# Two-layer decoder trunk: places of 96 and 64 slots in turn, and a branch for each overfull expert

## Chip, cores and metric

The kernel runs on one core of a Trainium2 chip. The metric is the device time of one execution in microseconds (us), the median of several runs. TensorE (PE) multiplies matrices, VectorE (DVE), ScalarE (ACT) and GpSimd (POOL) do the element-wise work, SyncE (SP) issues nearly all loads, and sixteen DMA engines move the data.

## What is computed

Two pre-norm residual layers over 256 tokens of width 1024, in float32. Layer 0 has two kinds of attention and a dense SwiGLU; layer 1 has sliding-window attention beside a short convolution, and then eight experts, of which each token takes two. The change touches only these experts:

```python
def moe_swiglu(x, w_router, w_gate, w_up, w_down):
    xt = x.reshape(B * S, D)
    logits = (xt @ w_router).astype(jnp.float32)
    top_vals, top_idx = lax.top_k(logits, TOP_K)
    top_w = jax.nn.softmax(top_vals, axis=-1)
    ...
    for e in range(N_EXPERTS):
        y = y + gates[:, e:e + 1] * swiglu(xt, w_gate[e], w_up[e], w_down[e])
```

Each expert has three matrices of 1024 x 3584 in float32. 256 tokens with two experts each make 512 pairs, 64 per expert on the mean.

## The kernel before

The first part (layer 0 and the attention of layer 1) is not touched. The last part, the expert stage, starts near 495 us and ends the program.

**Places.** The stage works through eight places, 0 to 7. A place has a fixed number of slots, `CAPS`: 96, 64, 96, 96, 64, 96, 96, 64. A slot is a column of a matrix into which a token is gathered. Expert 0 always has place 0; the other seven are ranked by their token counts on the chip (`arrange`), and `RANKS` tells which rank goes to places 1 to 7, so that the places of 64 get the smaller experts. `read_counts` loads into registers which expert stands in each place (on SyncE, for the addresses of the weights) and, on each engine, `t.over`, the largest number of tokens beyond a place's slots.

**Work of a place.** The place's tokens are gathered by a matmul with a one-hot matrix (L1090, tile tt). The hidden width of 3584 is done in two halves, r = 0 and 1. Each half takes two loads of the gate matrix, two of the up matrix (L1138, tile mm) and two of the down matrix (L1181 and L1185, tiles y and yo): twelve loads of 3584 KB per place. TensorE works on blocks of 32 slots, of which four matmuls stand side by side in its columns. A place of 96 has three blocks, a place of 64 two. In the down part the first two blocks go into y with 512 columns a matmul; the third goes into yo with 256, and a place of 64 has no yo. L1165 transposes the hidden values (once per half for the first two blocks, once more for the third), L1213 and L1214 scatter the result back to the tokens.

**Order.** `experts` writes a plan: gate of one half, then the down part of the half before, then up, with the small steps (gather of the next group, transposes, scatter) as fillers between. TensorE runs in just this order; the other engines' order is the scheduler's.

**Buffers.** All weights go through four raw buffers of 28 KB per partition, in turn. When TensorE has finished a load, the next is issued on SyncE's queue into the freed buffer, so at most four loads are under way or waiting to be used. The first four are issued before the stage starts.

**End.** After the last place come the final norm and two output transfers (L1285). Then stand two bodies behind branches (L1292): if `t.over` is above 0, all eight places are run again with 96 slots each for the tokens left over, and if it is above 96 once more.

Of the kernel before, what the change touches and what calls it, by code (L numbers as in the profile page):

```python
# [13 lines left out]
I32 = mybir.dt.int32  # L14
AF = mybir.ActivationFunctionType
OP = mybir.AluOpType
# [4 lines left out]
S = 256  # L21
NB = 2
FF = 3584
NE = 8
# [4 lines left out]
BIG = 7168  # L29
NPARTS = 3  # L30

CAPS = (96, 64, 96, 96, 64, 96, 96, 64)
RANKS = (4, 0, 1, 5, 2, 3, 6)


def _pieces(x, bits, n):
# [52 lines left out]
def trunk(ctx: ExitStack, tc: tile.TileContext, a: dict, out: bass.AP):  # L89
    nc = tc.nc  # L90
    V, A, G, T = nc.vector, nc.scalar, nc.gpsimd, nc.tensor
# [38 lines left out]
    turn = [0]  # L130
# [18 lines left out]
    def split(u):  # L149
        if u.load.view is None:  # L150
            load(u.load)
        v, n, w = u.load.view[:, u.j0:u.j0 + u.n], u.n, u.load.at[4]
        pool, size = parts, 2048
        hi, lo = (pool.tile([128, size], F32R, name=x)[:, :n * w].rearrange("p (k w) -> p k w", k=n)
                  for x in ("whi", "wlo"))
        A.activation(hi, v, AF.Copy)  # L156
        m = w - w // u.pool // 2 * 2 if w >= 256 else w
        V.tensor_tensor(lo[:, :, :m], v[:, :, :m], hi[:, :, :m].bitcast(F32), op=OP.subtract)  # L158
        if m < w:
            G.tensor_tensor(lo[:, :, m:], v[:, :, m:], hi[:, :, m:].bitcast(F32), op=OP.subtract)  # L160
        u.hl = (hi, lo)
# [6 lines left out]
    order = ExitStack()  # L168
# [74 lines left out]
    t = SimpleNamespace(pt=pt)  # L243
# [96 lines left out]
    def masks():  # L340
# [11 lines left out]
        for i in range(NE):  # L352
            G.memset(place[:, 0, i:i + 1], float(CAPS[i]))
            G.memset(place[:, 1, i:i + 1], float(RANKS[i - 1] if i else -1))
        V.tensor_tensor(lower, other.to_broadcast([128, NE, NE]), own.to_broadcast([128, NE, NE]), op=OP.is_lt)
# [104 lines left out]
    plan = []  # L460
# [496 lines left out]
    def arrange():  # L957
        rp, n = t.rp, NE - 1
        sq = [128, n, n]
        c = t.count[:, 1:]  # L960
        more, same = rp.tile(sq, F32, name="more"), rp.tile(sq, F32, name="same")
        own, other = c[:, :, None].to_broadcast(sq), c[:, None, :].to_broadcast(sq)
        V.tensor_tensor(more, other, own, op=OP.is_gt)
        V.tensor_tensor(same, other, own, op=OP.is_equal)
        V.tensor_tensor(same, same, lower[:, :n, :n], op=OP.mult)
        V.tensor_tensor(more, more, same, op=OP.add)
        rk = rp.tile([128, n], F32, name="rk")
        V.tensor_reduce(rk, more, axis=AX.X, op=OP.add)
        t.at = rp.tile(sq, F32, name="at")
        V.tensor_tensor(t.at, rk[:, None, :].to_broadcast(sq), place[:, 1, 1:, None].to_broadcast(sq), op=OP.is_equal)  # L970
        t.pos = placed(t.pos, "pos")
        ei = rp.tile([128, 2, NE], F32, name="ei")
        moved(ei[:, 0], slot[:, :NE])
        moved(ei[:, 1], t.count)
        V.tensor_tensor(ei[:, 1], ei[:, 1], place[:, 0], op=OP.subtract)
        t.most = rp.tile([128, NE + 1], I32, name="most")
        V.tensor_copy(t.most[:, :NE], ei[:, 0])
        V.tensor_reduce(ei[:, 0, 0:1], ei[:, 1], axis=AX.X, op=OP.max)
        V.tensor_scalar(t.most[:, NE:], ei[:, 0, 0:1], 0.0, None, op0=OP.max)

    def moved(o, x):
        n = NE - 1
        p = t.rp.tile([128, n, n], F32, name="moved", bufs=2)
        V.tensor_tensor(p, t.at, x[:, None, 1:].to_broadcast([128, n, n]), op=OP.mult)
        V.tensor_reduce(o[:, 1:], p, axis=AX.X, op=OP.add)
        V.tensor_copy(o[:, 0:1], x[:, 0:1])

    def placed(x, name):
        o = t.rp.tile([128, NB, NE], F32, name=name + "s")
        for b in range(NB):  # L990
            moved(o[:, b], x[:, b])
        return o
# [38 lines left out]
        t.ep = rpool(ctx, "ep", 2)  # L1031

    def read_counts():
        t.over = nc.values_load(t.most[0:1, NE:], min_val=0, max_val=S)
        t.ei = [None] + [nc.values_load(t.most[0:1, i:i + 1], engines=(mybir.EngineType.SP,), min_val=0, max_val=NE - 1,
                                        skip_runtime_bounds_check_because="sums of one index times 1 and others times 0")
                         for i in range(1, NE)]
# [9 lines left out]
    O, NG = 32, 3  # L1047
# [21 lines left out]

    weights = Weights()  # L1070

    def experts(base, caps, first=(), then=()):
        gath, d, dT = {}, {}, {}
        groups = ((0,), (1, 2), (3, 4), (5, 6), (7,))
        group = {s: (g, sum(caps[i] for i in g if i < s)) for g in groups for s in g}

        def dispatch(g):
# [147 lines left out]
        def steps_out(e, g, sizes=(7,)):  # L1225
            out_, j0 = [], 0
            for n in sizes:
                out_.append(do(down, e, part_out(e, g, j0, n), g, j0, n))
                j0 += n
            return out_  # L1230

        def outs(e, r, sizes):
            return steps_out(e, 2 * r) + steps_out(e, 2 * r + 1, sizes)

        plan = [*first, do(dispatch, groups[0])] + [do(gather, groups[0], k) for k in range(0, KD, 2)] + list(then)
        fill, waiting = [], []

        def put(steps):
            for x in steps:
                plan.append(x)  # L1240
                for _ in range(2 if len(fill) > 5 else 1):
                    if fill:
                        plan.append(fill.pop(0))

        for e in range(NE):
            for r in range(2):
                if r == 1 and e + 1 < NE and group[e + 1][0][0] == e + 1:
                    g = group[e + 1][0]
                    fill += [do(dispatch, g)] + [do(gather, g, k) for k in range(0, KD, 2)]
                if e == NE - 1 and r == 0:  # L1250
                    fill.append(do(final_gain))
                if r == 0:
                    fill.append(do(combine_T, e))
                put(steps_in("gate", e, r, "g") + [do(act1, e, r)])
                if waiting:
                    put(outs(*waiting.pop(0)))
                    if r == 0:
                        fill.append(do(part_y, e - 1))
                        fill += [do(scatter, e - 1, b) for b in range(NB)]
                put(steps_in("up", e, r, "u") + [do(act2, e, r)])  # L1260
                fill[:0] = [do(act_T, e, r, x) for x in range(caps[e] // O - 1)]
                last = (e, r) == (NE - 1, 1)
                waiting.append((e, r, (4, 2, 1) if last else (7,)))
        plan += fill + outs(*waiting.pop(0))
        e = NE - 1
        plan += [do(final_in), do(part_y, e)] + [do(scatter, e, b) for b in range(NB)]
        return plan + [do(final2, b) for b in range(NB)] + [do(final3, b) for b in range(NB)]

    def final_gain():
        t.gfin = row(a['final_norm'], D, "gfin", t.ep, bufs=1)  # L1270
# [11 lines left out]
    def final3(b):  # L1282
        f, o = t.fs[b], t.o[b]
        V.scalar_tensor_tensor(o, h[:, b], f[:, 3:4], t.gfin, op0=OP.mult, op1=OP.mult)
        (nc.sync, nc.scalar)[b].dma_start(out[0, b * 128:(b + 1) * 128], o)  # L1285

    mine = experts((0,) * NE, CAPS, [do(experts_open)], [do(order.close), do(in_order, 'PE'), do(arrange), do(gates),
                                                         do(read_counts)])
    execute(plan + mine)
    order.close()  # L1290
    for i in range(2):
        with tc.If(t.over > i * NG * O):  # L1292
            weights = Weights()
            turn[0] = 0
            more_ = experts([c + i * NG * O for c in CAPS], (NG * O,) * NE)
            for _ in range(4):
                weights.send()
            execute(more_)


_INS = ['x', 'positions', 'l0_norm_mix', 'l0_w_in', 'l0_b_forget', 'l0_q_norm', 'l0_w_q_up',
# [28 lines left out]
```

## Time and profile before

| What | us |
|---|---|
| median of 3 runs | 1384.11 (1382.22 to 1386.67) |
| the profiled execution, its time | 1382.37 |
| the profiled execution, its span | 1380.6 |
| TensorE busy in the span | 1320.4 |
| VectorE / ScalarE / GpSimd busy | 382.0 / 301.7 / 166.9 |
| expert stage, from the first gather to the span's end | 495 to 1380.6 |

The span runs from the first to the last instruction in the profile; the time has 1.8 us more around it. Busy time of TensorE counts matmuls that wait in its pipeline, so a full TensorE is read together with the DMA's rate. In rows of windows and of groups "x" is a count of instructions; a float32 matmul is listed as two, so 48 matmuls of the program are x96.

### The profile page before, as it was taken

To read this page: it belongs to the slowest core of one execution; us is meant where nothing else is said; L and a number is where in the kernel's file an instruction comes from. 1 tells how busy PE (TensorE), PEld (TensorE's weight loads), DVE (VectorE), ACT (ScalarE), POOL (GpSimd) and SP (SyncE) were. 2 spreads that over 40 slices of the span, in tenths; PEclk is the share of its full clock that TensorE was granted. 3 is DMA by queue.
4 is the path that set the end of the run, shared out by engine and by line. 5 is a ranking of instruction groups with operands and counts; after the bars stand their busy time and mean duration, and the time that the engine had idled before them with its cause. 6 is when DMAs were issued, how large, how long until landed. Compare 5 with 4: busy or idle time off the path is not lost.

```text
span 1380.6 us, 24882 instructions
## 1 busy us (share of the span) xinstructions
PE 1320.4 (96%) x11207; PEld 710.2 (51%) x11207; DVE 382.0 (28%) x713; ACT 301.7 (22%) x477; POOL 166.9 (12%) x117
## 2 busy tenths in 40 slices
PE   7999899999999999999899999999998999999994
PEld 6876788888888753433233433333432333343321
DVE  7566545555577530012001001101100100200202
ACT  6555533333345420000000101001001000100001
POOL 3312444444442100000000000000000000000000
PEclk9999999999999999999999999999999999999997
DMA  7622445555553689999999999999999999999993
GB/s 247 202 95 66 166 162 183 183 183 183 183 182 135 252 335 383 367 378 427 414 424 425 408 384 374 357 398 411 423 425 415 423 425 408 384 354 388 424 420 130
DMA packets 75817, 432.37 MB, mean 313 GB/s; under 512 B 3596, under 2 KB 7712, under 8 KB 71472
## 3 DMA queue, kind: packets, MB, share of 16 engines
q1 hardware_dynamic: 74992, 428.48, 79.2%
q8 instruction: 92, 1.51, 0.4%
q0 software_dynamic: 560, 1.62, 0.3%
q10 hardware_dynamic: 144, 0.52, 0.1%
q14 instruction: 29, 0.24, 0.1%
HBM read 429.57 MB, written 1.05 MB: 312 GB/s over the span
## 4 chain that ended last, share of the span: by engine, by line
PE 81%; DMA 9%; DVE 2%; ACT 1%; issue 1%; POOL 1%; POOLq 0%; ACTq 0%; SPq 0%; DVEq 0%
PE mm L1138 34%; PE y L1181 11%; PE mm L197 7%; PE mm L198 7%; PE mm L199 7%; DMA raw<-in_l_w_up_dram 6%; PE yo L1185 4%; DMA raw<-in_l_w_gate_dram 4%; PE tt L1090 2%; PE tt L1165 1%; PE ww L368 1%; PE ww L197 1%; PE ww L198 1%; PE ww L199 1%; PE mm L411 1%
## 5 line engine op out<-in xcount | busy, mean ns | idle before, releaser
L1138 PE MATMUL mm<-raw,g 128*32 128x448 f32 x5376 | 519.6, 544 | 13.3 <-DMA raw<-in_l_w_up_dram 11.0
L1138 PEld LDWEIGHTS mm<-raw,g 128*32 128x32 f32 x5376 | 173.6, 111 | 337.3 <-issue 313.1
L1181 PE MATMUL y<-raw,ehT 128*32 128x512 f32 x1792 | 220.0, 593 | 2.5 <-DMA raw<-in_l_w_down_dram 2.2
L160 POOL TENSOR_TENSOR wlo<-raw,whi 128x288 fp32r<-128x288 f32 (+6 forms) x74 | 153.7, 2077 | 286.1 <-ACT whi L156 265.8
L158 DVE TENSOR_TENSOR wlo<-raw,whi 128x1760 fp32r<-128x1760 f32 (+6 forms) x74 | 143.4, 1939 | 134.6 <-ACT whi L156 134.4
L156 ACT ACTIVATE whi<-raw 128x2048 fp32r<-128x2048 f32 (+4 forms) x74 | 134.4, 1817 | 154.4 <-PE mm L199 93.3
L199 PE MATMUL mm<-whi,xl 128*128 128x512 f32 (+3 forms) x352 | 136.0, 387 | 2.9 <-DVE xl L286 2.8
L197 PE MATMUL mm<-whi,xh 128*128 128x512 f32 (+3 forms) x352 | 137.8, 391 | 0.8 <-ACT xh L285 0.8
L198 PE MATMUL mm<-wlo,xh 128*128 128x512 f32 (+3 forms) x352 | 135.7, 386 | 0.0
L1166 ACT ACTIVATE ehT<-tt 64x256 f32<-64x256 f32 (+1 forms) x36 | 17.1, 475 | 475.5 <-PE tt L1165 475.3
L1280 POOL TENSOR_TENSOR fs<-fs,nhalf 128x1 f32<-128x1 f32 x2 | 1.1, 550 | 875.7 <-DVE fs L1279 875.7
L1152 DVE TENSOR_TENSOR hid<-hid,mm 128x448 f32<-128x448 f32 x42 | 26.1, 622 | 282.6 <-PE mm L1138 279.2
L1181 PEld LDWEIGHTS y<-raw,ehT 128*32 128x32 f32 x1792 | 56.1, 110 | 75.1 <-issue 48.8
L1185 PE MATMUL yo<-raw,ehT 128*32 128x256 f32 x1120 | 86.1, 379 | 0.0
L1185 PEld LDWEIGHTS yo<-raw,ehT 128*32 128x32 f32 x1120 | 36.4, 110 | 83.8 <-issue 82.5
L199 PEld LDWEIGHTS mm<-whi,xl 128*128 128x128 f32 x352 | 66.7, 189 | 18.1 <-DVE xl L286 4.6
L197 PEld LDWEIGHTS mm<-whi,xh 128*128 128x128 f32 x352 | 66.7, 190 | 16.0 <-ACT xh L285 1.7
L198 PEld LDWEIGHTS mm<-wlo,xh 128*128 128x128 f32 x352 | 66.7, 190 | 13.5 <-issue 0.6
L197 PE MATMUL mm<-xh,whi 128*128 128x256 f32 x160 | 46.8, 292 | 0.0
L1147 ACT ACTIVATE hid<-mm 128x448 f32<-128x448 f32 x42 | 22.9, 544 | 109.1 <-PE mm L1138 109.1
L198 PE MATMUL mm<-xl,whi 128*128 128x256 f32 x160 | 45.4, 284 | 0.0
L199 PE MATMUL mm<-xh,wlo 128*128 128x256 f32 x160 | 45.4, 284 | 0.0
(310 smaller groups left out, 1039.0 us busy)
## 6 DMA issues: line engine op xcount, KB each, us to landing
raw<-in_l_w_gate_dram SPq DMA_DIRECT2D x32, 3584.0 KB, 15.2
raw<-in_l_w_up_dram SPq DMA_DIRECT2D x32, 3584.0 KB, 17.8
raw<-in_l_w_down_dram SPq DMA_DIRECT2D x31, 3584.0 KB, 17.5
raw<-in_l_w_in_dram SPq DMA_DIRECT2D x15, 1024.0 KB, 5.2
raw<-in_l_w_down_dram SPq DMA_DIRECT2D x15, 1024.0 KB, 5.0
raw<-in_l_w_gate_dram SPq DMA_DIRECT2D x14, 1024.0 KB, 5.2
raw<-in_l_w_up_dram SPq DMA_DIRECT2D x14, 1024.0 KB, 5.1
raw<-in_l_w_out_dram SPq DMA_DIRECT2D x8, 1024.0 KB, 5.2
```

The lines of the kernel that those rows point to most:

```text
L156: A.activation(hi, v, AF.Copy)
L158: V.tensor_tensor(lo[:, :, :m], v[:, :, :m], hi[:, :, :m].bitcast(F32), op=OP.subtract)
L160: G.tensor_tensor(lo[:, :, m:], v[:, :, m:], hi[:, :, m:].bitcast(F32), op=OP.subtract)
L197: T.matmul(ps, l[0], r[0], start=first, stop=False, **kw)
L198: T.matmul(ps, l[0], r[1], start=False, stop=False, **kw)
L199: T.matmul(ps, l[1], r[0], start=False, stop=last, **kw)
L1090: T.matmul(p[:, k], t.xg[:, b, (k0 + k) * 128:(k0 + k + 1) * 128], d[g][:, b, :n], start=(b == 0), stop=(b == 1))
L1138: T.matmul(ps[key][j][i * O:(i + 1) * O], x[:, k0 + k, g * O:(g + 1) * O], w[:, k, c:c + CH], **at)
L1147: A.activation(x[:, g], ps["g"][g], AF.Silu)
L1152: V.tensor_tensor(x[:, g], x[:, g], ps["u"][g], op=OP.mult)
L1181: T.matmul(t.y[c * O:(c + 1) * O], x[:, (2 * i + c % 2) * O:(2 * i + c % 2 + 1) * O], w[:, j, c // 2 * 512:(c // 2 + 1) * 512], **at)
L1185: T.matmul(t.yo[c * O:(c + 1) * O], x[:, (4 + i) * O:(5 + i) * O], w[:, j, c * 256:(c + 1) * 256], **at)
```

## The change

The slots become 96, 64, 96, 64, 96, 64, 96, 64: place 3 has 64 instead of 96, place 4 has 96 instead of 64, and place 5 has 64 instead of 96. The ranks move with them: the three largest of experts 1 to 7 get places of 96, the other four get 64. The tile `most` gets eight further numbers, each place's own surplus. Behind the output stands one branch on the largest surplus; inside it each place has two bodies behind branches of their own, which run that place alone with 96 slots, and then the final norm and the output are done again.

```diff
-CAPS = (96, 64, 96, 96, 64, 96, 96, 64)
-RANKS = (4, 0, 1, 5, 2, 3, 6)
+CAPS = (96, 64, 96, 64, 96, 64, 96, 64)
+RANKS = (3, 0, 4, 1, 5, 2, 6)
...
         V.tensor_tensor(ei[:, 1], ei[:, 1], place[:, 0], op=OP.subtract)
-        t.most = rp.tile([128, NE + 1], I32, name="most")
+        t.most = rp.tile([128, 2 * NE + 1], I32, name="most")
+        V.tensor_scalar(t.most[:, NE + 1:], ei[:, 1], 0.0, None, op0=OP.max)
         V.tensor_copy(t.most[:, :NE], ei[:, 0])
         V.tensor_reduce(ei[:, 0, 0:1], ei[:, 1], axis=AX.X, op=OP.max)
-        V.tensor_scalar(t.most[:, NE:], ei[:, 0, 0:1], 0.0, None, op0=OP.max)
+        V.tensor_scalar(t.most[:, NE:NE + 1], ei[:, 0, 0:1], 0.0, None, op0=OP.max)
...
-    def experts(base, caps, first=(), then=()):
+    def experts(base, caps, groups, first=(), then=(), finish=()):
...
-    for i in range(2):
-        with tc.If(t.over > i * NG * O):
-            weights = Weights()
-            turn[0] = 0
-            more_ = experts([c + i * NG * O for c in CAPS], (NG * O,) * NE)
-            for _ in range(4):
-                weights.send()
-            execute(more_)
+    def rest(s, base):
+        nonlocal weights
+        weights = Weights()
+        turn[0] = 0
+        plan = experts({s: base}, {s: NG * O}, ((s,),))
+        for _ in range(4):
+            weights.send()
+        execute(plan)
+
+    with tc.If(t.over > 0):
+        final_gain()
+        for s in range(NE):
+            over = nc.values_load(t.most[0:1, NE + 1 + s:NE + 2 + s], min_val=0, max_val=S)
+            for i in range(2):
+                with tc.If(over > i * NG * O):
+                    rest(s, CAPS[s] + i * NG * O)
+        execute(finish)
```

**TensorE, place 3.** The rows are the second half's gate of place 3 and the down part that follows, before (mm is a bank of the gate or up product, raw a weight buffer, tt a bank of small work):

```order
L1138 MATMUL mm<-raw,g 32x448 x48
L1165 MATMUL tt<-ident,hid 128x128 x7
L1138 MATMUL mm<-raw,g 32x448 x48
L1165 MATMUL tt<-ident,hid 64x128 x7
L1181 MATMUL y<-raw,ehT 32x512 x4
L1185 MATMUL yo<-raw,ehT 32x256 x4
```

and now:

```order
L1138 MATMUL mm<-raw,g 32x448 x32
L1165 MATMUL tt<-ident,hid 128x128 x7
L1138 MATMUL mm<-raw,g 32x448 x32
L1181 MATMUL y<-raw,ehT 32x512 x56
L1138 MATMUL mm<-raw,g 32x448 x112
```

Each gate load is used by 32 matmuls instead of 48, the transposes of the third block are gone, and the down part is one run into y without the matmuls into yo that alternated with it. (The x112 holds the two up loads and the first gate load of place 4, which now has 48.)

**VectorE, routing before place 0.** ei holds the places' surplus, disp is a one-hot matrix, and the first g copy belongs to the gather of place 0. One piece of the difference:

```order
 L975 TENSOR_TENSOR ei<-ei,place 128x8
 L1082 TENSOR_SCALAR disp<-slot,poss 128x64
-L978 TENSOR_REDUCE ei<-ei 128x1
+L977 TENSOR_SCALAR most<-ei 128x8
 L1097 COPY g<-tt 128x192
-L979 TENSOR_SCALAR most<-ei 128x1
-L1009 RECIPROCAL tw<-tw 128x2
+L979 TENSOR_REDUCE ei<-ei 128x1
+L1010 RECIPROCAL tw<-tw 128x2
 L1082 TENSOR_SCALAR disp<-slot,poss 128x64
```

The new operation takes the reduction's place ahead of the copy, the reduction moves behind the copy, and the last write of `most` (L980 now) follows the second dispatch row.

**GpSimd, end of the program.** Every engine has the same branches there. Before:

```order
L1280 TENSOR_TENSOR fs<-fs,nhalf 128x1 x2
L1034 TENSOR_LOAD most
L1292 COMPARE_AND_BRANCH
L126 DMA gfin<-in_final_norm_dram 128x1024
L1280 TENSOR_TENSOR fs<-fs,nhalf 128x1 x2
L1292 UNCONDITIONAL_BRANCH
L1292 ISA
L1292 UNCONDITIONAL_BRANCH
L1292 COMPARE_AND_BRANCH
```

and now:

```order
L1280 TENSOR_TENSOR fs<-fs,nhalf 128x1 x2
L1035 TENSOR_LOAD most
L1303 COMPARE_AND_BRANCH
L126 DMA gfin<-in_final_norm_dram 128x1024
L1306 TENSOR_LOAD most
L1308 COMPARE_AND_BRANCH
```

Before, a second compare-branch stands behind the first body, at the program's top level. Now the inner ones stand within the body of the first.

## Rows read from the trace of the kernel before

**Rows 1.** The page, parts 1 and 2: busy time; GB/s in 40 slices.

```profile
PE 1320.4 (96%) x11207; PEld 710.2 (51%) x11207; DVE 382.0 (28%) x713; ACT 301.7 (22%) x477; POOL 166.9 (12%) x117
...
GB/s 247 202 95 66 166 162 183 183 183 183 183 182 135 252 335 383 367 378 427 414 424 425 408 384 374 357 398 411 423 425 415 423 425 408 384 354 388 424 420 130
```

**Rows 2.** Windows: length; PE, PEld, DVE, ACT, POOL busy; clock, DMA share, GB/s.

```profile
495.00:610.00 115.00, 113.65 (x1189) 46.56 (x1191) 12.62 (x61) 8.63 (x19) 0.00 (x0) 1.00 0.91 355
610.00:750.00 140.00, 130.81 (x1289) 46.48 (x1285) 16.53 (x31) 11.07 (x21) 0.00 (x0) 0.98 1.01 421
750.00:800.00 50.00, 49.68 (x538) 20.59 (x534) 2.24 (x6) 3.98 (x10) 0.00 (x0) 1.00 1.00 413
800.00:945.00 145.00, 143.56 (x1538) 54.63 (x1534) 16.22 (x32) 11.61 (x23) 0.00 (x0) 1.00 0.95 379
945.00:1150.00 205.00, 200.47 (x2057) 74.68 (x2053) 20.38 (x36) 13.54 (x27) 0.00 (x0) 1.00 1.01 422
1150.00:1275.00 125.00, 123.78 (x1328) 48.93 (x1324) 13.42 (x26) 11.19 (x23) 0.00 (x0) 1.00 0.95 380
1275.00:1345.00 70.00, 66.84 (x677) 23.73 (x673) 7.68 (x13) 4.51 (x8) 0.00 (x0) 0.98 1.01 422
```

**Rows 3.** The page, part 6: DMA issues, KB each, median us to landing.

```profile
raw<-in_l_w_gate_dram SPq DMA_DIRECT2D x32, 3584.0 KB, 15.2
```

**Rows 4.** The chain of work that ended last: start us, us, what.

```profile
561.24 0.86 PE y L1181 x8
...
562.53 0.86 PE y L1181 x8
...
647.22 6.15 PE mm L1138 x64
...
660.58 6.05 PE y L1181 x56
...
749.63 9.16 PE mm L1138 x96
...
1317.32 20.91 DMA raw<-in_l_w_up_dram
```

**Rows 5.** Windows, instructions of tile tt alone: PE, PEld, DVE, ACT busy.

```profile
610.00:1300.00 690.00, 56.67 (x305) 40.06 (x305) 32.86 (x64) 19.25 (x47) 1.00 0.99 404
```

**Rows 6.** Line L1112 in 690:755, 755:800 and 800:880, in this order: issue to landing.

```profile
DMA to landing us min/median/max: 25.2/27.1/28.7
DMA to landing us min/median/max: 13.8/16.3/20.0
DMA to landing us min/median/max: 11.4/12.3/13.9
```

**Rows 7.** Timeline of VectorE near 499 us; then line L1034 (ns, start us).

```profile
499.20 0.14 DVE L979 TENSOR_SCALAR most<-ei 128x1 int32<-128x1 f32 x1
499.26 0.15 DVE L1009 RECIPROCAL tw<-tw 128x2 f32<-128x2 f32 x1
499.33 0.23 DVE L1082 TENSOR_SCALAR disp<-slot,poss 128x64 f32<-128x64 f32 x1
...
L1034 PEldq TENSOR_LOAD <-most x1: 484/484/484, 499.4 to 499.4; - x1
```

**Rows 8.** Line L1292: duration ns min/median/max, first and last start us.

```profile
L1292 SPq EVENT_SEMAPHORE  x16: 17/17/17, 1372.9 to 1378.9; - x16
L1292 SPq COMPARE_BRANCH  x2: 50/52/53, 1369.4 to 1375.5; - x2
...
L1292 DVEq EVENT_SEMAPHORE  x2: 21/21/21, 1374.9 to 1378.6; - x2
```

**Rows 9.** Windows around two waits in place 1, columns as in group 2.

```profile
675.00:682.00 7.00, 4.56 (x52) 1.63 (x48) 0.00 (x0) 0.00 (x0) 0.00 (x0) 1.00 1.02 421
682.00:687.00 5.00, 5.00 (x36) 1.56 (x40) 0.00 (x0) 0.00 (x0) 0.00 (x0) 0.66 1.01 412
726.00:731.00 5.00, 4.20 (x28) 1.29 (x32) 1.29 (x2) 0.66 (x2) 0.00 (x0) 0.66 1.02 420
```

More of the change, by code (lines that the diff above doesn't have):

```diff
@@ L1033, in read_counts @@
     def read_counts():
-        t.over = nc.values_load(t.most[0:1, NE:], min_val=0, max_val=S)
+        t.over = nc.values_load(t.most[0:1, NE:NE + 1], min_val=0, max_val=S)
         t.ei = [None] + [nc.values_load(t.most[0:1, i:i + 1], engines=(mybir.EngineType.SP,), min_val=0, max_val=NE - 1,
@@ L1070, in trunk @@
     weights = Weights()
-    def experts(base, caps, first=(), then=()):
+    def experts(base, caps, groups, first=(), then=(), finish=()):
         gath, d, dT = {}, {}, {}
-        groups = ((0,), (1, 2), (3, 4), (5, 6), (7,))
         group = {s: (g, sum(caps[i] for i in g if i < s)) for g in groups for s in g}
@@ L1243, in put @@
                         plan.append(fill.pop(0))
-        for e in range(NE):
+        prev = None
+        order_ = sorted(group)
+        for e, after in zip(order_, order_[1:] + [None]):
             for r in range(2):
-                if r == 1 and e + 1 < NE and group[e + 1][0][0] == e + 1:
-                    g = group[e + 1][0]
+                if r == 1 and after is not None and group[after][0][0] == after:
+                    g = group[after][0]
                     fill += [do(dispatch, g)] + [do(gather, g, k) for k in range(0, KD, 2)]
-                if e == NE - 1 and r == 0:
-                    fill.append(do(final_gain))
                 if r == 0:
+                    if after is None and finish:
+                        fill.append(do(final_gain))
                     fill.append(do(combine_T, e))
@@ L1257, in experts @@
                     if r == 0:
-                        fill.append(do(part_y, e - 1))
-                        fill += [do(scatter, e - 1, b) for b in range(NB)]
+                        fill.append(do(part_y, prev))
+                        fill += [do(scatter, prev, b) for b in range(NB)]
                 put(steps_in("up", e, r, "u") + [do(act2, e, r)])
                 fill[:0] = [do(act_T, e, r, x) for x in range(caps[e] // O - 1)]
[L1262 to L1267, printed above, removed]
+                waiting.append((e, r, (4, 2, 1) if after is None and r == 1 else (7,)))
+            prev = e
+        plan += fill + outs(*waiting.pop(0)) + list(finish[:1])
+        return plan + [do(part_y, prev)] + [do(scatter, prev, b) for b in range(NB)] + list(finish[1:])
     def final_gain():
@@ L1285, in final3 @@
         (nc.sync, nc.scalar)[b].dma_start(out[0, b * 128:(b + 1) * 128], o)
-    mine = experts((0,) * NE, CAPS, [do(experts_open)], [do(order.close), do(in_order, 'PE'), do(arrange), do(gates),
-                                                         do(read_counts)])
+    finish = [do(final_in)] + [do(final2, b) for b in range(NB)] + [do(final3, b) for b in range(NB)]
+    mine = experts((0,) * NE, CAPS, ((0,), (1, 2), (3, 4), (5, 6), (7,)), [do(experts_open)],
+                   [do(order.close), do(in_order, 'PE'), do(arrange), do(gates), do(read_counts)], finish)
     execute(plan + mine)
     order.close()
-    for i in range(2):
-        with tc.If(t.over > i * NG * O):
-            weights = Weights()
-            turn[0] = 0
-            more_ = experts([c + i * NG * O for c in CAPS], (NG * O,) * NE)
-            for _ in range(4):
-                weights.send()
-            execute(more_)
+    def rest(s, base):
[14 more added lines that the diff above has]
+        execute(finish)
 _INS = ['x', 'positions', 'l0_norm_mix', 'l0_w_in', 'l0_b_forget', 'l0_q_norm', 'l0_w_q_up',
```

## The prediction

> **What bounds the kernel now.** The page comes first: TensorE is busy for 96% of the span, so it looks like the bound, yet the GB/s line stands over 400 in most slices of the second half [rows 1]. Two engines that are both nearly full call for a table by stage. Cutting the expert stage into windows shows two kinds of stretch [rows 2]. In 610 to 750, 945 to 1150 and 1275 to 1345 us the DMA moves 421 to 422 GB/s and TensorE has gaps. In 800 to 945 and 1150 to 1275 us TensorE is full (143.56 of 145 us) and the DMA falls to 379 and 380 GB/s. The reader is to see that the bound changes sides, and that the slow-DMA stretches are just those in which two places of 96 slots stand in a row (places 2 and 3, and 5 and 6).
>
> The weights set a floor that no slot count moves. One load is 3584 KB [rows 3], 3.670 MB, so at 422 GB/s it takes 8.70 us, and the twelve loads of a place take 104.4 us. TensorE's need depends on the slots. One gate or up load costs it 9.16 us with 96 slots and 6.15 us with 64; one down load costs 7 x 1.29 = 9.03 us with 96 (seven pairs of wide and narrow matmuls, 1.29 us from one pair's start to the next) and 6.05 us with 64 [rows 4]. The small work on the tt banks (gathers, transposes, scatters) is 56.67 us in 690 us [rows 5], which at 850/8 = 106 us a place is 6.5 places and 8.7 us each. So a place of 96 needs 8 x 9.16 + 4 x 9.03 + 8.7 = 118.1 us and a place of 64 needs 8 x 6.15 + 4 x 6.05 + 8.7 = 82.1 us, against the DMA's 104.4.
>
> How far TensorE may lag before the DMA runs dry is read from the time from issue to landing, since four buffers rotate and a load is issued when TensorE frees one [rows 6]. With TensorE starved (690 to 755) the longest is 28.7 us; at the end of the first place of 96 (755 to 800) the shortest is 13.8 us and the rate is still 413 GB/s; one step later (800 to 880) it is 11.4 to 13.9 and the rate is 379. So the buffers hold about 28.7 - 13.8 = 14.9 us of lag. One place of 96 lags 118.1 - 104.4 = 13.7 us and just fits. Two in a row lag 27.4, of which 12.5 must come back as idle DMA. Measured against 422 GB/s: 800 to 945 loses (422 - 379)/422 x 145 = 14.8 us, 1150 to 1275 loses (422 - 380)/422 x 125 = 12.4 us, and 750 to 800 loses (422 - 413)/422 x 50 = 1.1 us. Sum 28.3 us. The start (495 to 610, 355 GB/s) loses 18.3 us more.
>
> **The change part by part.** *Places.* Place 3 becomes 64 slots, place 4 becomes 96, place 5 becomes 64; one block of 32 slots less in all. Places 0 to 2 and 7 are untouched, so the 18.3 us of the start stay. TensorE loses 8 x (9.16 - 6.15) + 4 x (9.03 - 6.05) = 36.0 us and about 2 us of transposes, 38 us; but that is not the gain, since the DMA's bytes stay. Now every place of 96 stands between two of 64. Each 64 regains 104.4 - 82.1 = 22.3 us, more than the 13.7 of the 96 before it, so the buffers are drained again at the start of each 96 and TensorE waits some 8.6 us per pair. The two stretches of 14.8 and 12.4 us go. What is late next is the DMA itself, for all of 612 to the last landing. The 1.1 us of place 2's end stands once more for each of places 4 and 6: 28.3 - 3 x 1.1 = 25.0 us gained. Bounds: 28.3 if no such end costs anything; 21.7 if each costs twice as much. I take 25.0, by the row of 750 to 800, the only single 96 that the trace shows followed by another place.
>
> *Routing.* One more small VectorE operation (the per-place surplus), put ahead of the reduction; that reduction now stands behind the copy of the gather, and a 64-slot dispatch row stands ahead of the last `most`. TensorE's register load of `most` waits for it: it began at 499.4, right behind `most` at 499.20 + 0.14 [rows 7]. The reduction and the reciprocal take 0.06 to 0.07 us each from start to start, the dispatch row at most 0.23: 0.3 us on the path, for behind that load stand TensorE's first expert matmuls, and place 0 is bound by TensorE. SyncE waits for the same value, with four loads already under way. Bounds 0 and 0.6 us.
>
> *The end.* Before, two branches are taken past two bodies; each engine jumps twice. SyncE's compare-branches start at 1369.4 and 1375.5, and its next instructions, waits on semaphores, start at 1372.9 and end with the one at 1378.9; VectorE's wait comes at 1374.9 and again at 1378.6 [rows 8]. Only the second jump lies behind the landing of the output. After, one compare-branch on the whole surplus skips everything, so the second jump, 1378.6 - 1375.5 = 3.1 us, goes; I take 2.9 us, since a few waits may move behind the landing. Bounds 0 (if the longer skip costs more) and 3.1. The bodies in the branch are not run: the router of the reference on its own inputs gives the eight experts 58, 62, 69, 65, 61, 61, 72 and 64 tokens. Expert 0 keeps place 0; by size the others are 72, 69, 65 (places of 96) and 64, 62, 61, 61 (places of 64). All fit, the fourth with no slot to spare.
>
> *Other engines.* ACT and VectorE lose one third block of copies per load group; they are busy 11.61 and 16.22 us of 145 [rows 2], so nothing is priced there. The order of loads on SyncE's queue is as before.
>
> **Sum.** 25.0 - 0.3 + 2.9 = 27.6 us. The profiled execution took 1382.37 us (span 1380.6), so 1354.8; the median of the runs is 1.74 us above it, 1384.11, so 1356.5 us on that scale.
>
> **A rule weighed.** The stretches at 379 and 380 GB/s could be read as the memory's own limit, and those at 421 to 422 say that they are not [rows 2]. The Trainium skill's page "DMA: Bandwidth & Descriptors", section "Where 436 GB/s comes from", holds that for transfers from HBM to SBUF the HBM side binds, at about 358 GB/s for a core. By that a load would take 10.25 us and a place 123 us, an estimate from that page, more than TensorE's need in any place, and the change would give only its end. This trace differs, with stretches of 421 to 422 GB/s, and the measurement decides; what is left of it is rival (2).
>
> **The rivals.** (1) *A single 96 doesn't fit.* The margin is 14.9 - 13.7 = 1.2 us. After a wait TensorE ran at half clock for part of the next stretch: it is busy 4.56 of 7 us in 675 to 682, and then the granted clock is 0.66 in 682 to 687, as again in 726 to 731 [rows 9]; that is 5 x 0.34 = 1.7 us of work lost each time at 1.2 instead of 2.4 GHz. There will be more waits, so more of this; at two per pair it is 3.4 us, inside the 8.6 us of waiting. Against the rival: place 2 had both dips and lost 1.1 us. If places 4 and 6 each lose half of what the second 96 lost, 6.2 us instead of 1.1, the gain falls by 10.2 us: 1366.7. The Trainium skill's "TensorE: Matmul & The Clock Gate", section "HAM oscillation", tells of a matmul loop that falls back to half clock at every wait for a tile; this trace agrees in kind, with the two stretches at 0.66.
>
> (2) *The DMA is at its limit anyway*, and 379 to 380 is what it can do beside a full TensorE. Then only the end gains: 1384.1 - 2.6 = 1381.5, within 0.3%. Against it: in 945 to 1150 TensorE is busy 200.47 of 205 us and the rate is 422 [rows 2].
>
> (3) *TensorE was the only bound*, and its 38 us come back whole with the 2.6: 1343.5. That needs a DMA faster than 422 in every window; the page's slices reach 425 to 427 and no more [rows 1].
>
> (4) *The surplus branch runs* (slower). It decides at one token: if the kernel's arithmetic sends a single token more to the expert with 64, a place overflows. Then, behind the finished output, twelve loads come in with nothing to overlap, 11.4 + 11 x 8.70 = 107 us [rows 3, 6], a tail as now follows the last landing, 1380.6 - 1338.2 from the last up load to the end less two down loads of 8.70, 25 us [rows 4], and the fifteen branches not taken cost up to 3 us each: some 177 us, 1533 us. Against it: in the reference the closest token at which that expert stands third is behind by 0.031 at a logit of 14.3, far for arithmetic split into high and low parts.
>
> **How the numbers follow.** Forecast 0.72, (1) 0.15, (2) 0.03, (3) 0.06, (4) 0.04. The likeliest gives 1356.5. Its own bounds: best 28.3 + 3.1 = 31.4 us less, 1352.7; worst 21.7 - 0.6 + 0 = 21.1, 1363.0. The range reaches to (1), and 2.7 us below the best for a DMA that is a little faster when never idle: 1350 to 1367; (2), (3) and (4), 0.13, are left out. A measurement tells about 0.3%, 4 us, from no change. Faster 0.72 + 0.15 + 0.06 = 0.93, same 0.03, slower 0.04.
>
> **What would show it.** Right: in windows from about 612 us to the last landing the DMA stays at 415 GB/s or more, with no 100-us stretch under 400; the last up load lands at about 1313 instead of 1338.2; issue to landing doesn't fall under 13 us except in the first place; TensorE's busy share falls by about 1%, with more waits for raw; one compare-branch per engine at the end. Wrong by (1): windows at the ends of places 4 and 6 (about 1000 and 1210 us) under 400 GB/s, or more stretches at half clock. Wrong by (4): a further set of weight loads behind the output.

## The result, and the profile after

| | before | after |
|---|---|---|
| median (range), us | 1382.74 (1381.05 to 1386.67) | 1360.39 (1355.87 to 1364.90) |
| ratio, 95% interval | | 0.983 (0.981 to 0.986) |
| the profiled execution, us | 1382.37 | 1357.23 |
| its span, us | 1380.6 | 1355.5 |

The change makes the kernel 1.7% faster, 22 us by the medians and 25.1 us by the two profiled executions; the forecast was 27.6. The time lies inside the range.

The page after, parts 1 and 2, answers to [rows 1]: busy time, and GB/s in 40 slices.

```profile
PE 1287.0 (95%) x10713; PEld 695.3 (51%) x10713; DVE 377.4 (28%) x704; ACT 298.5 (22%) x471; POOL 166.9 (12%) x117
...
GB/s 251 197 89 63 169 185 186 186 187 186 184 142 172 184 345 372 366 363 423 419 429 414 424 397 412 423 425 418 423 416 406 424 418 424 427 410 399 425 424 150
```

TensorE has lost 33.4 us of busy time (38 were forecast), the span 25.1. The slices at 374, 357, 384 and 354 of before are gone; the lowest of the stage's second part are 397 and 399.

Windows of after, which answer to [rows 2] (length; PE, PEld, DVE, ACT, POOL busy; clock, DMA share, GB/s):

```profile
495.00:610.00 115.00, 113.35 (x1187) 45.95 (x1189) 11.88 (x54) 8.63 (x19) 0.00 (x0) 1.00 0.90 356
610.00:750.00 140.00, 132.12 (x1301) 46.94 (x1297) 16.93 (x31) 11.07 (x21) 0.00 (x0) 0.98 1.01 423
750.00:800.00 50.00, 49.68 (x532) 20.60 (x525) 1.82 (x5) 3.98 (x10) 0.00 (x0) 1.00 1.00 416
800.00:900.00 100.00, 94.73 (x979) 35.26 (x982) 11.36 (x21) 6.95 (x13) 0.00 (x0) 1.00 1.00 412
900.00:1000.00 100.00, 95.90 (x963) 36.17 (x959) 10.00 (x19) 8.21 (x17) 0.00 (x0) 0.98 1.01 422
1000.00:1100.00 100.00, 96.89 (x991) 36.48 (x987) 11.36 (x21) 7.45 (x15) 0.00 (x0) 0.99 1.00 415
1100.00:1200.00 100.00, 93.75 (x919) 34.17 (x915) 9.03 (x15) 7.98 (x16) 0.00 (x0) 0.97 1.01 422
1200.00:1275.00 75.00, 75.00 (x828) 29.59 (x824) 6.77 (x14) 5.54 (x11) 0.00 (x0) 1.00 1.00 408
```

No window behind 610 us is under 408 GB/s, where before had 379 and 380. The prediction's sign of 415 or more is missed in two of them, 412 and 408; that of no 100 us under 400 is met. The start, place 0, is as it was: 356 against 355. TensorE now has gaps in every pair of places but is full at the end of each place of 96 (75.00 of 75 us in the last row).

The gate and up loads, line L1112, in 690:755, 755:800 and 800:880, from issue to landing, answer to [rows 6]:

```profile
DMA to landing us min/median/max: 24.8/26.5/29.0
DMA to landing us min/median/max: 14.4/17.0/20.6
DMA to landing us min/median/max: 14.7/17.2/25.2
```

The first two rows are like those of before. The third had 11.4/12.3/13.9 before, the mark of a DMA that has nothing queued. Now the loads begin to queue up again there, since place 3 has 64 slots.

The chain that ended last, after (start us, us, what), its weight loads from place 1 on:

```profile
666.12 23.43 DMA raw<-in_l_w_gate_dram
...
698.96 25.95 DMA raw<-in_l_w_up_dram
...
877.88 25.21 DMA raw<-in_l_w_gate_dram
...
914.20 23.44 DMA raw<-in_l_w_up_dram
...
1088.91 25.47 DMA raw<-in_l_w_gate_dram
...
1125.49 24.86 DMA raw<-in_l_w_up_dram
...
1294.14 23.11 DMA raw<-in_l_w_up_dram
```

Once per pair of places the chain now passes through two loads. The last up load lands at 1294.14 + 23.11 = 1317.25, against 1317.32 + 20.91 = 1338.23 before [rows 4]: 21.0 us of the 25.1 are there by then. Start and duration of the three up loads give landings at 724.91, 937.64 and 1150.35, that is 212.7 us from a load to the same load two places on.

**A ledger of landings.** The stage's 96 weight loads can be counted by their landing, issue time plus time to landing in the trace. (The very last goes in three pieces, so the queue has 98.) The table gives the time from one mark to the next, twelve loads each in the order of the queue (one place's worth of bytes), for before, after and the kernels of the next section. Each mark is the last down load of a place: the 14th load is place 0's, and the columns end with those of places 2 to 6.

| kernel | 14th lands at | 27-38 | 39-50 | 51-62 | 63-74 | 75-86 | sum | last up load lands |
|---|---|---|---|---|---|---|---|---|
| before | 612.4 | 106.6 | 117.4 | 105.7 | 105.7 | 115.3 | 550.6 | 1338.2 |
| end only | 616.3 | 106.4 | 117.9 | 105.4 | 105.5 | 115.7 | 551.0 | 1342.3 |
| after | 610.6 | 107.1 | 105.6 | 107.1 | 105.6 | 105.5 | 531.0 | 1317.2 |
| after again | 613.6 | 106.1 | 105.5 | 108.3 | 105.6 | 105.5 | 531.1 | 1319.6 |
| places only | 618.4 | 107.8 | 105.7 | 106.9 | 105.7 | 106.6 | 532.5 | 1326.1 |
| waits filled | 617.0 | 105.7 | 105.6 | 110.6 | 105.6 | 105.5 | 532.9 | 1324.9 |
| pairs in a row | 612.4 | 105.6 | 105.6 | 117.0 | 105.6 | 105.5 | 539.2 | 1325.4 |
| place 0 with 64 | 597.4 | 105.5 | 105.6 | 105.6 | 105.5 | 105.5 | 527.8 | 1301.7 |
| all 64 | 599.4 | 105.5 | 104.4 | 105.2 | 105.5 | 105.6 | 526.2 | 1300.6 |
| 64 first, 96 last | 597.5 | 105.5 | 105.6 | 105.5 | 105.6 | 105.5 | 527.7 | 1301.8 |

The floor is 105.5 us for twelve loads. Before exceeds it in two places, by 11.9 and 9.8 us. After exceeds it by 1.6 twice. The 25.1 us of the profiled executions are 1.8 in the first 26 loads, 550.6 - 531.0 = 19.6 in the next 60, -0.5 from there to the last up load, and 42.4 - 38.3 = 4.1 from that landing to the span's end.

### The profile page after: what moved, and what is told of

Read it like the earlier page. It is cut to its first block, busy times and chain, and to the rows that moved or that the text cites. A ratio compares the mean times of both kernels' runs of the same rounds, so it can differ in the third digit from the quotient of the medians.

```text
span 1355.5 us, 23874 instructions
## 1 busy us (share of the span) xinstructions
PE 1287.0 (95%) x10713; PEld 695.3 (51%) x10713; DVE 377.4 (28%) x704; ACT 298.5 (22%) x471; POOL 166.9 (12%) x117
## 4 chain that ended last, share of the span: by engine, by line
PE 77%; DMA 13%; DVE 2%; ACT 1%; issue 1%; POOL 1%; POOLq 0%; ACTq 0%; SPq 0%; DVEq 0%
PE mm L1138 31%; PE y L1181 9%; DMA raw<-in_l_w_up_dram 8%; PE mm L197 7%; PE mm L198 7%; PE mm L199 7%; DMA raw<-in_l_w_gate_dram 6%; PE yo L1185 4%; PE tt L1090 2%; PE ww L368 1%; PE tt L1165 1%; PE ww L199 1%; PE ww L197 1%; PE ww L198 1%; PE mm L411 1%
## 5 line engine op out<-in xcount | busy, mean ns | idle before, releaser
L1138 PE MATMUL mm<-raw,g 128*32 128x448 f32 x5120 | 501.2, 548 | 27.8 <-DMA raw<-in_l_w_up_dram 20.3
L1138 PEld LDWEIGHTS mm<-raw,g 128*32 128x32 f32 x5120 | 168.1, 111 | 340.1 <-issue 314.3
L1181 PE MATMUL y<-raw,ehT 128*32 128x512 f32 x1792 | 214.8, 593 | 0.9 <-DMA raw<-in_l_w_down_dram 0.6
L1166 ACT ACTIVATE ehT<-tt 128x512 f32<-128x512 f32 (+1 forms) x32 | 15.6, 487 | 459.7 <-PE tt L1165 459.6
L198 PEld LDWEIGHTS mm<-wlo,xh 128*128 128x128 f32 x352 | 66.7, 190 | 13.3 <-issue 0.5
L1185 PE MATMUL yo<-raw,ehT 128*32 128x256 f32 x896 | 68.9, 379 | 0.0
L1185 PEld LDWEIGHTS yo<-raw,ehT 128*32 128x32 f32 x896 | 29.1, 110 | 67.0 <-issue 66.6
L1097 DVE COPY g<-tt 128x192 f32<-128x192 f32 (+1 forms) x16 | 4.6, 321 | 162.0 <-PE tt L1090 162.0
## 6 DMA issues: line engine op xcount, KB each, us to landing
raw<-in_l_w_up_dram SPq DMA_DIRECT2D x32, 3584.0 KB, 20.6
```

The lines of the kernel that those rows point to most:

```text
L198: T.matmul(ps, l[0], r[1], start=False, stop=False, **kw)
L1138: T.matmul(ps[key][j][i * O:(i + 1) * O], x[:, k0 + k, g * O:(g + 1) * O], w[:, k, c:c + CH], **at)
L1166: copy = V.tensor_copy if j0 else lambda a_, b_: A.activation(a_, b_, AF.Copy)
L1181: T.matmul(t.y[c * O:(c + 1) * O], x[:, (2 * i + c % 2) * O:(2 * i + c % 2 + 1) * O], w[:, j, c // 2 * 512:(c // 2 + 1) * 512], **at)
L1185: T.matmul(t.yo[c * O:(c + 1) * O], x[:, (4 + i) * O:(5 + i) * O], w[:, j, c * 256:(c + 1) * 256], **at)
```

## The experiments

Two theories were set against each other. By the **buffer theory**, that of the prediction, the DMA is the bound, and time is lost only where TensorE's lag exceeds what four buffers hold; so the order of the slots counts. By the **work theory** the amount of TensorE's work counts, and the change gains because a block of 32 slots is gone. Ratios are against the kernel before on the same chip (medians 1383.65, 1383.21 and 1383.11 us in the three groups).

### The two parts apart

Places alone, in the kernel before with its old end:

```diff
-CAPS = (96, 64, 96, 96, 64, 96, 96, 64)
-RANKS = (4, 0, 1, 5, 2, 3, 6)
+CAPS = (96, 64, 96, 64, 96, 64, 96, 64)
+RANKS = (3, 0, 4, 1, 5, 2, 6)
```

> The new slots and ranks with the old end of the program (two branches, each past a body of all eight places). Buffer theory (the gain is the DMA that no longer runs dry behind two places of 96 in a row, about 19 to 21 us between the two traces): 1362 to 1364 us, that is 19 to 21 us under the kernel before. If the end of the program gave more than the 3 to 4 us that its rows show, the time lies above 1366.

Measured: 1363.08 us, ratio 0.9845 (0.9815 to 0.9875), 20.6 us less. The other part alone is the kernel after with the two old lines:

```diff
-CAPS = (96, 64, 96, 64, 96, 64, 96, 64)
-RANKS = (3, 0, 4, 1, 5, 2, 6)
+CAPS = (96, 64, 96, 96, 64, 96, 96, 64)
+RANKS = (4, 0, 1, 5, 2, 3, 6)
```

> The old slots and ranks with the new end (one branch on the largest surplus, the bodies of single places inside it) and the new number in the routing. By the rows of the end (34.5 us from the last weight issue to the last instruction before, 30.5 us after) 3 to 4 us under the kernel before: 1379. If the jump costs the same however many branches there are: 1382 to 1383.

Measured: 1379.07 us, ratio 0.9966 (0.9945 to 0.9987), 4.6 us less. And the kernel after, unaltered, beside them:

> The changed kernel unaltered, on the same chip as the others, for its spread: its six runs lay between 1355.9 and 1364.9 us, with a granted clock of 0.987 in the shortest and 0.981 in the longest. Theory that half-clock stretches at the start of a place of 96 cost time: again a spread of 5 us or more, longer with a lower clock. Theory that the spread was one of chips: all runs here within 2 us.

Measured: 1358.23 us, ratio 0.9806 (0.978 to 0.9832), 25.4 us less. Its six runs spread by 3.1 us, between what the two theories on the spread asked for, so they decide nothing on it. As for the parts, 20.6 + 4.6 = 25.2: they add up. In the end-only kernel both dips are back, as its windows show (columns as above):

```profile
750.00:800.00 50.00, 49.30 (x510) 20.71 (x506) 5.79 (x11) 3.98 (x10) 0.00 (x0) 1.00 1.01 417
800.00:900.00 100.00, 99.09 (x1046) 37.66 (x1042) 12.68 (x24) 8.79 (x17) 0.00 (x0) 1.00 0.94 369
...
1200.00:1275.00 75.00, 74.68 (x796) 30.20 (x792) 4.97 (x11) 5.98 (x13) 0.00 (x0) 1.00 0.91 362
```

### Same work, other order

The slots of after, but with those of places 2 and 3 exchanged, so that places 3 and 4 have 96 in a row:

```diff
-CAPS = (96, 64, 96, 64, 96, 64, 96, 64)
-RANKS = (3, 0, 4, 1, 5, 2, 6)
+CAPS = (96, 64, 64, 96, 96, 64, 96, 64)
+RANKS = (3, 4, 0, 1, 5, 2, 6)
```

> As the changed kernel, four places of 96 and four of 64, but in another order: 96, 64, 64, 96, 96, 64, 96, 64. TensorE's work is the same. Buffer theory: places 3 and 4 are two of 96 in a row, the second costs 12 to 15 us of idle DMA, less the 2 us that the single one cost: 1370 to 1373 us. Theory that only the amount of TensorE's work counts: 1360 us, as the changed kernel.

Measured: 1367.37 us, ratio 0.9893 (0.9862 to 0.9924). The same slots, moved, give back 9 us of the 25 by the medians, 12 by the ratios. Its windows at the pair:

```profile
800.00:900.00 100.00, 98.78 (x1031) 35.72 (x1027) 7.79 (x13) 7.70 (x15) 0.00 (x0) 1.00 1.01 421
900.00:1000.00 100.00, 98.78 (x1052) 38.03 (x1045) 12.54 (x24) 9.28 (x19) 0.00 (x0) 1.00 0.97 398
1000.00:1100.00 100.00, 99.09 (x1039) 38.44 (x1041) 11.91 (x23) 7.44 (x15) 0.00 (x0) 1.00 0.97 394
```

TensorE is as full in the first row as in the others; only the lag that it has gathered differs. In the ledger the loss stands in one place, loads 51 to 62, with 117.0 - 105.5 = 11.5 us. The work theory gave no loss here, and the time measured lies a little below the range of the buffer theory.

### Less work, and the floor

Place 0 with 64 slots and three places of 96 (one block less than after; by the counts of the prediction all tokens still fit):

```diff
-CAPS = (96, 64, 96, 64, 96, 64, 96, 64)
-RANKS = (3, 0, 4, 1, 5, 2, 6)
+CAPS = (64, 96, 64, 96, 64, 96, 64, 64)
+RANKS = (0, 3, 1, 4, 2, 5, 6)
```

> Place 0 has 64 slots and there are three places of 96, each between two of 64: 64, 96, 64, 96, 64, 96, 64, 64. All tokens of these inputs fit. Buffer theory: the start, where the DMA lost 18.3 us because place 0 with 96 slots held its buffers, loses only some 6: about 1348 us. Work theory (one block of 32 slots less gave 22 us, so one more gives as much): 1338 us. If the start is bound by the first loads and not by the slots: 1358 to 1360.

Measured: 1340.75 us, ratio 0.9694 (0.9671 to 0.9718), 42.5 us less than before and some 15 to 18 less than after in its repetition (by the ratios and by the medians): with the next, the best of all. By itself this lies nearer to the 1338 of the work theory than to the 1348 of the buffer theory. The next kernel decides between them: all places with 64, as a measure only, since it leaves out tokens.

```diff
-CAPS = (96, 64, 96, 64, 96, 64, 96, 64)
-RANKS = (3, 0, 4, 1, 5, 2, 6)
+CAPS = (64, 64, 64, 64, 64, 64, 64, 64)
+RANKS = (0, 1, 2, 3, 4, 5, 6)
...
-    with tc.If(t.over > 0):
+    with tc.If(t.over > 100):
```

> All eight places have 64 slots and the branch for the surplus is never taken, so the tokens beyond 64 of three experts are left out; the loads are unchanged. It measures the floor of the DMA. Buffer theory: as the kernel with 64 slots in place 0, less the ends of the places of 96 (2 to 2.5 us each): about 1341 us. Work theory: four blocks less than the changed kernel at 22 us each, 1272 us.

Measured: 1340.19 us, ratio 0.9694 (0.9663 to 0.9725), the same. Three blocks of 32 slots less bring nothing more; by the work theory's numbers they were worth 66 us. What the buffer theory had wrong in the kernel before this one is the start: it left some 6 us of loss there, but with 64 slots in place 0 the start is nearly on the floor as well. One row of windows of each: the start of the kernel with 64 slots in place 0, then all 64 over 710 us:

```profile
505.00:610.00 105.00, 99.10 (x982) 35.52 (x975) 6.77 (x16) 10.14 (x20) 0.00 (x0) 1.00 0.98 408
```

```profile
600.00:1310.00 710.00, 589.54 (x5238) 199.98 (x5234) 57.61 (x100) 41.95 (x84) 0.00 (x0) 0.94 1.01 421
```

With all 64, TensorE idles for 120 of 710 us and the DMA moves 421 GB/s: this is the floor of the weights. The kernel with place 0 of 64 stands on it from the start, 408 GB/s in 505 to 610, where after has 356 over the same stretch. Its chain shows the pairs on the floor too:

```profile
754.26 28.44 DMA raw<-in_l_w_gate_dram
...
965.36 28.45 DMA raw<-in_l_w_gate_dram
...
1176.45 28.44 DMA raw<-in_l_w_gate_dram
```

These loads land at 782.70, 993.81 and 1204.89: 211.1 us from a place to the second next, against 212.7 of after.

### A place of 96 at the end

If place 0 should have 64, the 96 may go last:

```diff
-CAPS = (96, 64, 96, 64, 96, 64, 96, 64)
-RANKS = (3, 0, 4, 1, 5, 2, 6)
+CAPS = (64, 96, 64, 96, 64, 96, 64, 96)
+RANKS = (0, 4, 1, 5, 2, 6, 3)
```

> Four places of each kind, 64 first: 64, 96, 64, 96, 64, 96, 64, 96. As with 64 in place 0 and three places of 96, 1341 us at the last landing, but TensorE ends 13.7 us of lag behind in the last place of 96: 1352 to 1358 us. If the order did not matter: 1358, as the changed kernel; if the last place's lag is hidden: 1341.

Measured: 1359.05 us, ratio 0.9844 (0.9818 to 0.9871), no better than after. That is 1 us above the range expected, and the time alone can't tell it from the theory that the order doesn't matter (1358); the profiled execution, 1356.57, lies inside. The trace decides. In the ledger its loads are on the floor throughout, and its last up load lands at 1301.8, as early as with place 0 of 64. But its span ends at 1354.7, 52.9 us behind that landing, where after has 38.3. TensorE's lag of the last place has no load to hide behind: 14.6 us more, near the 13.7 worked out for one 96.

### Half clock at the waits

Rival (1) rested in part on TensorE at half clock after each wait. Here eight idle matmuls stand ahead of each load that TensorE waits for, so that it is busy while it waits:

```diff
+        def warm(n):
+            p = tbank().rearrange("p a c -> p (a c)")
+            for _ in range(n):
+                T.matmul(p[:, 0:256], onesb, onesb[:, None, :].to_broadcast([128, 2, 128]), start=True, stop=True)
...
+            if finish and ((caps[e] == 64 and key == "u" and r == 1) or (e and caps[e] == 96 and r == 0)):
+                warm(8)
...
+            if finish and caps[e] == 64 and r == 1 and e < NE - 1:
+                warm(8)
```

> The changed kernel with eight idle matmuls (128x256, bf16, into a bank that nobody reads) ahead of each load that TensorE waits for by the trace: up of the second half and down of places of 64, first gate and up of places of 96; about 0.9 us each, 7 us per pair of places, inside 8.6 us of waiting. If the half-clock stretches cost time: fewer of them, 1355 to 1357 us and a narrow spread. If they are hidden by the waits: 1360, as the changed kernel. If the fill delays TensorE at the start of a place of 96: 1363 or more.

Measured: 1363.13 us, ratio 0.9836 (0.981 to 0.9862), 4.9 us longer by the medians than after in its repetition (the intervals of the two ratios overlap), which is the third of the outcomes expected. One row of windows over 710 us, of after and then of this kernel:

```profile
600.00:1310.00 710.00, 680.68 (x6894) 254.43 (x6890) 72.45 (x134) 53.47 (x107) 0.00 (x0) 0.99 1.00 417
```

```profile
600.00:1310.00 710.00, 695.08 (x7073) 267.58 (x7065) 74.31 (x137) 53.47 (x107) 0.00 (x0) 1.00 1.00 414
```

The clock goes from 0.99 to 1.00, the rate doesn't rise, and the ledger has 532.9 us for the 60 loads, against 531.0 and 531.1; the loss is in one column, 51-62, with 110.6. So filling the dips bought nothing. It can't price them, though, since the idle matmuls cost TensorE time of their own. The kernel with all 64 can: its mean clock is 0.94 and it stands on the floor, so where the DMA sets the pace throughout, the dips cost nothing. In after they can cost no more than the 3.2 us by which its 60 loads exceed the floor.

### The branch taken

Exchanging the ranks of places 1 and 6 puts 65 tokens on a place of 64, one too many, so that the body of place 1 runs:

```diff
-RANKS = (3, 0, 4, 1, 5, 2, 6)
+RANKS = (2, 0, 4, 1, 5, 3, 6)
```

> The changed kernel with the ranks of places 1 and 6 exchanged, so that the expert with 65 tokens stands in a place of 64: one token is over and the branch of place 1 runs. By the prediction's price of its slower rival, 177 us (twelve loads of 8.70 us with a first of 11.4, a tail of 25 us, fifteen branches not taken at up to 3 us): 1535 us. If branches not taken cost next to nothing: 1490 us.

Measured: 1553.48 us, ratio 1.1238 (1.1213 to 1.1264), 195 us above after. Its windows behind the first output:

```profile
1345.00:1360.00 15.00, 6.12 (x29) 6.15 (x30) 3.44 (x6) 1.17 (x4) 1.12 (x3) 0.50 0.52 175
1360.00:1380.00 20.00, 13.59 (x127) 4.69 (x130) 0.36 (x1) 0.38 (x1) 0.00 (x0) 0.82 1.02 422
1380.00:1480.00 100.00, 99.13 (x1096) 36.86 (x1092) 6.25 (x12) 5.96 (x12) 0.00 (x0) 1.00 0.84 348
1480.00:1510.00 30.00, 7.01 (x52) 2.89 (x44) 8.76 (x14) 4.63 (x8) 1.10 (x2) 0.61 0.13 42
1510.00:1553.00 43.00, 0.00 (x0) 0.00 (x0) 0.00 (x0) 0.00 (x0) 0.00 (x0) 0.50 0.04 6
```

In the third row TensorE is the bound, not the DMA: the body runs with 96 slots. In the last row nothing works at all. Line L1308, the inner branches, tells who is late (duration ns min/median/max, first and last start us):

```profile
L1308 PEldq COMPARE_BRANCH  x17: 70/4504/5625, 1343.3 to 1546.6; - x17
L1308 DVEq COMPARE_BRANCH  x17: 47/56/67, 1348.8 to 1498.6; - x17
...
L1308 SPq COMPARE_BRANCH  x17: 38/45/50, 1349.2 to 1479.9; - x17
...
L1308 PEldq EVENT_SEMAPHORE  x15: 51/51/51, 1347.3 to 1551.2; - x15
```

On SyncE and VectorE a compare-branch takes about 0.05 us and the last one lies before 1500 us. On TensorE's queue its median is 4.5 us, and it walks through the bodies that are not taken until 1551.2. The same slots and ranks with the old end, which runs all eight places again:

```diff
-CAPS = (96, 64, 96, 96, 64, 96, 96, 64)
-RANKS = (4, 0, 1, 5, 2, 3, 6)
+CAPS = (96, 64, 96, 64, 96, 64, 96, 64)
+RANKS = (2, 0, 4, 1, 5, 3, 6)
```

> The same slots and ranks, one token over, with the old end: the body of all eight places runs again with 96 slots each, 8 x 118.1 us of TensorE's work by the prediction's price of a place of 96, and the tail: about 1363 + 970 = 2330 us.

Measured: 2343.89 us, ratio 1.6957 (1.692 to 1.6994). With one token too many the new end saves 790 us.

## Where the prediction was right, and where not

**The bound changes sides: right.** Once the bytes set the pace, less TensorE work gives nothing (all 64 and place 0 with 64 agree within 1 us), so TensorE's 38 us were not the gain. Rival (3), 1343.5 us, falls with that. Rival (2) falls because the windows at 379 and 380 became windows at 408 and more, one of them beside a TensorE that is busy 75.00 of 75 us. The rule weighed in the prediction, a limit of about 358 GB/s, does not hold for this kernel. The Trainium skill's page "HBM Reference", section "Specifications (TRN2)", says that a core which streams alone gets about 425 GB/s and that the lower figure is its share when both cores of a pair stream; the windows at 421 to 423 agree with that.

**The loss stands behind two 96 in a row: right.** Pairs in a row shows it with the work held constant.

**Its size: wrong, and that is the step that failed.** The term of 25.0 us for the places came out at 20.6 in places only (19.6 in the ledger of after), and the last up load landed at 1317.25 instead of about 1313. "Measured against 422 GB/s", the two stretches were to be worth 14.8 + 12.4 = 27.2 us. The ledger has 11.9 + 9.8 = 21.7. Half of the fault is in the yardstick: 422 is a window's rate, and 8.70 us per load and 104.4 per place were taken from it. Counted by landings, a place that is never short takes 105.5 us, which is 417 GB/s, and against that the same two rows give 13.3 + 11.2 = 24.5. The other 2.8 us are between two ways of counting, bytes within a window and whole loads landed, and were not followed up. Windows of a DMA that is never short read about 1% above the landings (421 against 417 GB/s in 620 to 1300 of the kernel with place 0 of 64), while the same stretch of before doesn't (404 against 403); why is open. Put into the prediction's own formula, 105.5 gives a lag of 118.1 - 105.5 = 12.6 us for a 96, and for two in a row 25.2 - 14.9 = 10.3 us lost instead of 12.5. The five pairs in the ledger (two in before, two in the end-only kernel, one in pairs in a row) lost 11.9, 9.8, 12.4, 10.2 and 11.5 us: three between the two values, two just below, on the mean 11.2.

**What a single 96 costs: right in the sum, not place by place.** Forecast 3 x 1.1 = 3.3 us. Against the floor of 527.8 after loses 3.2 in the 60 loads, after again 3.3, places only 4.7. But places 2, 4 and 6 did not lose 1.1 each: in after they lost 1.6, 1.6 and nothing, in its repetition 0.6, 2.8 and nothing, so that the sum fits so closely is partly luck. Rival (1), with 6.2 us for each of places 4 and 6, falls: without the idle matmuls the most that one lost is 2.8.

**The start untouched: right**, 356 against 355 GB/s. Of its price of 18.3 us, 64 slots in place 0 gave back 13.2: the place's last down load landed at 597.4 instead of 610.6.

**Issue to landing not under 13 us: nearly.** The gate and up loads stay at 14 us or more, but the prediction had looked at L1112 alone. The down loads come at the point of greatest lag, and one of place 2's end took 12.5 us.

**Half clock, rival (1): present, and not seen to cost.** The dips came, as told. The kernel with all 64 has the most of them and stands on the floor, and after is 3.2 us above it; filling them gained nothing.

**The end: right in kind, too small.** Forecast 2.9 - 0.3 = 2.6 us; measured 4.1 in the profile and 4.6 (1.8 to 7.6 by the interval) in the end-only kernel. Before, the second output lands at 1375.4, SyncE then meets its second compare-branch [rows 8], and the span ends 5.1 us behind the landing. After has one compare-branch on SyncE at line L1303, ahead of the landing:

```profile
L1303 SPq EVENT_SEMAPHORE  x9: 17/17/17, 1351.9 to 1353.7; - x9
...
L1303 DVEq EVENT_SEMAPHORE  x2: 21/21/21, 1354.0 to 1354.1; - x2
...
L1303 PEldq COMPARE_BRANCH  x1: 3404/3404/3404, 1344.0 to 1344.0; - x1
L1303 SPq COMPARE_BRANCH  x1: 53/53/53, 1348.4 to 1348.4; - x1
...
L1303 DVEq COMPARE_BRANCH  x1: 72/72/72, 1350.1 to 1350.1; - x1
```

Here the second output lands at 1353.7 and the span ends 1.7 us later. So the second jump, with the waits behind it, was worth 3.4 us and not 2.9. In places only, which has the old end, it is 5.1 us too, and 1.7 to 1.8 in the seven other kernels with the new end whose branch is not taken. The other 0.7 us, of which nothing was forecast, is the output transfer itself, which took 4.5 us from issue to landing before and 3.8 after; why is open. The routing's 0.3 us can't be told apart from this: TensorE's load of `most` began at 498.8, against 499.4 before [rows 7], within the spread of the part ahead.

**The branch: right on the point, too cheap.** One token decides, as rival (4) says, and the token counts hold, since no inner branch ran in after. The price was put at 177 us and is 195. From the first load behind the output (issued at 1355.8) to the last landing (1466.1) it took 110.4 us, where 107 had been put. Two terms behind that were too small. The tail of 25 us was read from a kernel whose last place has 64 slots; the body runs with 96, and TensorE's last matmul ends 23.2 us behind the last landing, against 10.9 in after. And the branches not taken cost more than 3 us each: two stand ahead of the body, and the thirteen behind it keep TensorE's queue from that last matmul to the end, 63.1 us, with the second final norm and output done beside them. That is 110.4 + 23.2 + 63.1 = 196.7 us, and the span is 196.9 us longer than after's.

**The median.** The profiled execution came 2.4 us above its forecast of 1354.8, the median 3.9 above 1356.5. The runs of after spread by 9 us. Part of such a spread lies ahead of the expert stage, in work that the change doesn't touch: in 105 to 117 us the granted clock was 1.00 in the profile of after (first row of windows) and 0.57 in that of places only (second), whose 14th load lands 7.8 us later.

```profile
105.00:117.00 12.00, 12.00 (x69) 7.72 (x68) 8.89 (x27) 7.10 (x24) 0.80 (x1) 1.00 0.01 1
```

```profile
105.00:117.00 12.00, 11.99 (x44) 7.96 (x44) 7.77 (x21) 4.76 (x13) 0.80 (x1) 0.57 0.01 1
```

In the same 12 us TensorE got through 44 instead of 69 matmuls. How much of the 9 us this is was not tried.

## What to carry to other kernels

Where two engines take turns as the bound, the order of heavy and light pieces counts, and the question is how much lag the buffers between them hold: put a light piece behind each heavy one, a light one first, where nothing is stored up yet, and a light one last, where nothing follows to hide the lag. Take the floor of a stream from the distance of landings, many loads apart, and not from a window's rate: 1% of it was a tenth of the gain forecast here. And a body behind a branch that is never taken still has its price in jumps, so put one test in front of all of them.

## What the runs showed of the hardware

A branch that skips a long body costs some 3 to 4 us on a queue: on SyncE 3.5 us from the compare-branch at 1348.4 to the next instruction at 1351.9, on VectorE 3.9 from 1350.1 to 1354.0; on GpSimd only 0.2, from 1348.6 to 1348.8. GpSimd has only a few instructions in the bodies it skips; whether that is the reason was not tried. The Trainium skill's page "Runtime: NRT & Kernel Launch", section "Instruction fetch mechanics", says that a taken branch whose target isn't in the current window makes the engine fetch it first, and gives no price; the trace agrees in kind: while TensorE's queue walks through its last thirteen bodies with the branch taken, 1488 to 1552 us, the DMA queue for instructions moves 26 packets of 16 KB, about two per body. That TensorE's queue shows the time in the compare-branch itself, 3.4 us here and 4.5 us at the median with the branch taken, while SyncE and VectorE show it behind theirs, was not expected, nor that TensorE alone holds up the end for over 40 us. VectorE's skips are shorter in that kernel, 0.2 to 1.7 us from a compare-branch to the wait behind it.

Even in kernels whose DMA is never short, a few landings come late: 24 loads take 211.1 us in the kernel with place 0 of 64, and most landings there are 8.5 to 8.8 us apart with two of 10.0 to 10.2 per 24 loads, always the same loads. The trace has something that goes with it: the DMA queue for instructions moves one packet of 16 KB every 10 to 23 us. In the three kernels that are never short (place 0 of 64, all 64, 64 first and 96 last) there are 19 landings between the 14th load and the last up load that come 9.6 us or more behind the one before, and each of them waits through the start of one of these packets: from one late landing to the next it is always exactly eight packets on. With place 0 of 64 that is every 10 to 15 loads, with all 64, where TensorE has fewer instructions per load, every 15 or 16. No run changes the instruction fetches alone, so a cause is not shown.
